# Folding the pooling branch's two weights into one, built on chip and kept in DRAM

## The chip, the cores and the metric

One core of a Trainium2 chip runs the whole model layer. The metric is the device time of one execution in microseconds. Of the kernel before, three runs are shown: 2617.74, 2624.07 and 2628.94, median 2624.07 us.

The engines are named as in the profile: PE (TensorE, matmuls; PEld its weight loads), DVE (VectorE), ACT (ScalarE), POOL (GpSimd) and SP (SyncE, which here only issues transfers). A name with a q behind it, such as SPq or ACTq, is the engine's instruction queue, where transfers are issued.

## The reference

The layer has two mixing branches, a gate on each, an output projection and a feed-forward part. Only the pooling branch changes. Cut to what matters (`u_pool` are the first 512 columns of the input projection, `zg` the gate columns):

```
# pool_mixer: for each of four groups of 128 channels, window w = 2, 4, 8, 16
outs.append(win_sum / count - ug[:, :, g])          # trailing mean minus token
mixed = einsum('bsgc,gcd->bsgd', pooled, pool_w)    # one 128x128 weight per group
mixed = mixed.reshape(B, S, 512) * pool_scale       # one scale per channel
ya = mixed @ w_pa                                   # 512 -> 1024
merged = gates[0] * ya + gates[1] * yb
x = x + merged @ w_o
x = x + conv_glu_ffn(rmsnorm(x))
```

Between the pooled channels and `ya` everything is linear: a block-diagonal 512x512 weight, a scale per channel, and a 512x1024 weight.

## The kernel before

**Precision and operands.** All inputs are 32-bit floats. A product is made of three matmuls in the fp32r type: each factor is split into a high part (a cast, on ACT) and a low part (the difference, on DVE), and high x high, high x low and low x high are accumulated. Activations are split by `split` (L591; cast L597, difference L598). Weights run through `Stream`: an operation of the plan takes one or more raw 256 KB loads (`load`, L176, issued by SP at L182 into 8 buffers, `N_RAW`), may add some of them (in the first mixer, sums of quarters of a weight, on POOL and DVE at L338 and L397), and then converts the result into a high and a low half (`convert`, cast L205 on ACT, difference L206 on DVE) in one of 6 operand buffers (`N_OPS`). `advance` runs the conversions ahead, one at each tick (six counted matmuls, L145), at most four operands (`LOOKAHEAD`) beyond the next to be used. A raw buffer is loaded again only when the last operation that reads it has been converted (`load_ahead`). Sums that the second mixer needs again are stored to DRAM (`keep`, stored at L310 by SP).

**Order of the work.** The sequence of 2048 tokens is worked in two passes of 1024 tokens, each of two blocks of 512. Each pass is `mixer` and then `ffn`. The large products use a seven-product scheme over 2x2 blocks (P1 to P7), with sums of weights and of activations as operands; the activations' forms (B11, T1, T2 and so on) are made by `forms_a_task` and `forms_b_task`, with transposes on PE (L646) and combinations on DVE (L703). `mixer` begins with `proj_io` (inputs and output gates of the recurrent branch), whose products go in the order P1, P2, P6, P5, P7, P4, P3 with four operands each and twelve matmuls per operand. P1 and P2 need one load per operand and no sums; in the first pass P6 needs three loads and two adds per operand (w8 to w11 in the profile's names). P6 needs the form T2, which is made from about P2 on. Then follow 14 units of `PROJ`: kinds fq, g and u, seven operands each. The tasks of the recurrent branch (HGRN) and of pooling run beside them, stepped by the ticks.

**The pooling branch.** The units ("u", 0) and ("u", 1) give the pooled channels' inputs. For each block and group a `pool_task` (L757) makes the windowed mean minus the token into `p` (L774 to L777), splits it (`pl`), multiplies it with the group's 128x128 part of `pool_wt` in three matmuls (L782 to L784) into a PSUM bank `pm`, evicts the bank with the scale on ACT (L786, `mx`) and spills it to DRAM (`md`, by ACT's queue at L791). `pool_wt` is one operand of the stream ("pw"), loaded in each pass before ("u", 0) and held until eight tasks are done. Near the end of the mixer `pa_task` fetches the eight tiles back (L796, by SP), splits them, and `branch("pa", ...)` multiplies them with eight operands of `w_pa` (256 KB each), gates and sums.

**Who orders what.** Each engine works its instructions in order. The program is written in the order described, and a scheduler orders each engine's instructions by a simulated timeline before the run, so an instruction that is ready may stand ahead of one written earlier. Queues are in order: a store that waits on SP holds the loads behind it.

Of the kernel before, what the change touches and what calls it, by code (L numbers as in the profile page):

```python
# [11 lines left out]
F32 = mybir.dt.float32  # L12
F32R = mybir.dt.float32r
U8 = mybir.dt.uint8
AF = mybir.ActivationFunctionType
# [3 lines left out]
P = 128  # L19
SEQ = 2048  # L20
D = 1024
KD = D // P
# [35 lines left out]
M_ORDER = (0, 4, 1, 5, 2, 6, 3, 7)  # L58
# [20 lines left out]
def tile_trunk(  # L79
# [3 lines left out]
    w_in_t: bass.AP,  # L83
    w_io: bass.AP,
    pool_wt: bass.AP,
    w_pa_t: bass.AP,
    w_pb_t: bass.AP,
    w_o: bass.AP,
    w_up_t: bass.AP,
# [6 lines left out]
    pe, act, dve, pool, sp = nc.tensor, nc.scalar, nc.vector, nc.gpsimd, nc.sync  # L96
# [6 lines left out]
    dram = ctx.enter_context(tc.tile_pool(name="dram", bufs=1, space=bass.MemoryType.DRAM))  # L103
    banks = ctx.enter_context(tc.tile_pool(name="banks", bufs=8, space=bass.MemoryType.PSUM))

    def slot(name, cols=TB, dt=F32):
        return slots.tile([P, cols], dt, tag="s", name=name, padded_shape=[P, 528])

    def bank(name, cols=512):
        return banks.tile([P, cols], F32, tag="b", name=name, padded_shape=[P, 512])  # L110

    def f32(ap):
        return ap.bitcast(F32)
# [30 lines left out]
    def mm(*args, **kw):  # L144
        count[1] = pe.matmul(*args, **kw)  # L145
        count[0] += 1
        if count[0] % MM_PER_TICK == 0:
            tick()
# [102 lines left out]
    stream = Stream()  # L251
# [60 lines left out]
    def plan_one(key, src):  # L312
        r = stream.raw(src)
        stream.op(key, lambda nm, r=r: r.tile, [r])
# [3 lines left out]
    def plan_io(b0):  # L318
        for p in IO_ORDER:
            for k in range(4):  # L320

                q = [w_io[k, :, c * 512 : (c + 1) * 512] for c in (0, 3, 1, 2)]
                one = {"P1": 0, "P2": 1, "P4": 3}
                if p in one:
                    plan_one("io", q[one[p]])
                    continue
                if b0:
                    plan_one("io", lambda k=k, p=p: kept["io", k, p])
                    continue
                use = {"P6": (2, 3, 0), "P5": (2, 3), "P7": (2, 0), "P3": (2, 3, 0, 1)}[p]  # L330
                raws = [stream.raw(q[i]) for i in use]

                def fn(nm, k=k, p=p, raws=raws):
                    t = raws[0].tile
                    for i, r in enumerate(raws[1:]):
                        t2 = slot(f"{nm}s{i}")
                        (dve if i == (p == "P6") and p != "P5" and p != "P7" else pool
                         ).tensor_tensor(t2, t, r.tile, ALU.add)  # L338
                        t = t2
                    keep(("io", k, p), t)  # L340
                    return t

                stream.op("io", fn, raws)

    def plan_unit(key, src, kind, i, order, b0):
        mv, mg = proj_tiles(kind, i)
# [8 lines left out]
    def plan_mixer(b0):  # L355
        plan_io(b0)
        for kind, i in PROJ:
            if (kind, i) == ("u", 0):
                plan_one("pw", pool_wt)
            plan_unit("in", w_in_t, kind, i, ORDER, b0)  # L360
        for key, src in (("pa", w_pa_t), ("pb", w_pb_t)):
            for i in range(8):
                plan_one(key, src[i // 2][:, i % 2 * 512 : i % 2 * 512 + 512])
        plan_rows("wo", w_o, R_OUT, KD // 2)

    def proj_tiles(kind, i):
# [155 lines left out]
    o_n1, o_n2, o_bg, o_ps, o_lb, o_hg, o_cb, o_cw = offs  # L522
# [8 lines left out]
    def col(o):  # L531
        return cols[:, o : o + 1]
# [58 lines left out]
    def split(src, name, on_pool=False):  # L591
        hi = slot(name + "h", TB, F32R)
        lo = slot(name + "l", TB, F32R)
        if on_pool:
            pool.tensor_scalar(hi, src, 1.0, 0.0, ALU.mult, ALU.add)
        else:
            act.copy(hi, src)  # L597
        dve.tensor_tensor(lo, src, f32(hi), ALU.subtract)  # L598
        return hi, lo
# [154 lines left out]
        return forms[key]  # L754


    def pool_task(b, g, u, w_mix, md):  # L757
        add = pool if g % 2 == 0 else dve
        w = WINDOWS[g]
        pool.tensor_copy(u[:, 1:16], uhist[:, g, 1:16])  # L760
        pool.tensor_copy(uhist[:, g, 1:16], u[:, 513:528])
        s = u
        k = 1
        lo = 1
        while k < w:
            t = slot(f"s{b}_{g}_{k}", 528)
            lo += k
            a = 16 if 2 * k == w else lo
            add.tensor_tensor(t[:, a:528], s[:, a:528], s[:, a - k : 528 - k], ALU.add)
            s = t  # L770
            k *= 2
            yield 6
        p = slot(f"p{b}_{g}")
        dve.scalar_tensor_tensor(p, s[:, 16:528], 1.0 / w, u[:, 16:528], ALU.mult, ALU.subtract)  # L774
        if b == 0:
            dve.tensor_tensor(p[:, :16], s[:, 16:32], inv[:, g], ALU.mult)
            dve.tensor_tensor(p[:, :16], p[:, :16], u[:, 16:32], ALU.subtract)  # L777
        pl = split(p, f"pl{b}_{g}")
        yield 6
        ps = bank(f"pm{b}_{g}")  # L780
        c = g * P
        pe.matmul(ps, w_mix[:, 0, c : c + P], pl[0], start=True, stop=False)  # L782
        pe.matmul(ps, w_mix[:, 0, c : c + P], pl[1], start=False, stop=False)
        pe.matmul(ps, w_mix[:, 1, c : c + P], pl[0], start=False, stop=True)  # L784
        t = slot(f"mx{b}_{g}")
        act.activation(t, ps, AF.Copy, scale=col(o_ps + g))  # L786
        md[b, g] = spill(t, f"md{b}_{g}")

    def spill(t, name):
        d = dram.tile([P, TB], F32, tag=name, name=name)  # L790
        act.dma_start(d, t)  # L791
        return d
# [307 lines left out]
    def proj_io(b0, forms, late, vd, zd):  # L1100
        bk = {}
        e1, u2, u3 = {}, {}, {}

        def temp(d, key, j):
            d[j] = slot(f"io{b0}_{key}_{j}")
            return d[j]

        def out_v(hf, j, a):
            t = slot(f"v{b0}_{hf}_{j}")
            value(t, a, bk["Y" if hf == 0 else "V"][j])  # L1110
            sp.dma_start(vd[hf][:, j, :], t)

        def out_z(hf, j, a):
            t = slot(f"z{b0}_{hf}_{j}")
            g = slot(f"zs{b0}_{hf}_{j}")
            value(t, a, bk["Z" if hf == 0 else "V"][j])
            act.activation(g, t, AF.Sigmoid)
            (dve if hf == 0 else pool).tensor_tensor(t, t, g, ALU.mult)
            sp.dma_start(zd[hf][:, j, :], t)

        def after(p, j):
            if p == "P1":
                act.copy(temp(e1, "e1", j), bk["X"][j])
            elif p == "P2":
                out_v(0, j, (e1[j], "add"))
            elif p == "P6":
                dve.tensor_tensor(temp(u2, "u2", j), e1[j], bk["Z"][j], ALU.subtract)
            elif p == "P7":
                dve.tensor_tensor(temp(u3, "u3", j), bk["Z"][j], e1[j], ALU.subtract)
                out_z(1, j, (u3[j], "add"))  # L1130
            elif p == "P4":
                out_z(0, j, (e1[j], "from"))
            elif p == "P3":
                out_v(1, j, (u2[j], "sub"))

        for p in IO_ORDER:
            xs = need(forms, FORM[p], late)
            kb = "Y" if p == "P2" else BANK[p]
            if kb not in bk:
                bk[kb] = [bank(f"io{b0}_{kb}_{j}") for j in range(NT)]  # L1140
            for k in range(4):
                if (p, k) == GO_IO[b0 > 0]:
                    go_io[0] = True
                w = stream.get("io")
                for j in range(NT):
                    n_step(bk[kb][j], w, xs[k], j, p in FIRST + ("P2",) and k == 0, k == 3,
                           skip_group_check=True)
                    if k == 3:
                        after(p, j)
                stream.used(1)  # L1150

    def mixer(b0, forms, late):
        vd = [dram.tile([P, NT, 512], F32, tag=f"vd{b0}_{hf}", name=f"vd{b0}_{hf}")
# [3 lines left out]
        md, od, gd = {}, {}, {}  # L1157
# [37 lines left out]
            return emit  # L1195

        held = {}
        pooled = [0]

        def pool_run(hf, g, u):  # L1200
            def gen():
                yield from pool_task(b0 + hf, g, u, held["w"], md)
                pooled[0] += 1
                if pooled[0] == 8:
                    stream.used(1)
            Task(gen())

        def emit_u(i):
            def emit(s, hf, a, ps):
# [44 lines left out]
        emits = {"fq": emit_fq, "u": emit_u, "g": emit_g}  # L1254
        mixed, oT = {}, {}
        for n, (kind, i) in enumerate(PROJ):
            if (kind, i) == ("u", 0):
                held["w"] = stream.get("pw")
            u = Unit(f"{kind[0]}r{b0}_{i}", "in", emits[kind](i))
            for p in ORDER:  # L1260
                u.multiply(p, forms, late)
                u.after(p)
                if n == len(PROJ) - 1 and p == "P1":
                    mtask = Task(pa_task())
# [318 lines left out]
```

## Time and profile before

| what | value |
|---|---|
| median of the three runs | 2624.07 us |
| lowest, highest | 2617.74, 2628.94 us |
| the profiled execution, its own time | 2626.91 us |
| its span | 2625.2 us |
| PE busy | 2537.5 us, 97% of the span, 11464 matmuls and transposes |
| DVE busy | 1977.9 us, 75% |
| ACT, POOL busy | 1170.8 us, 45%; 913.0 us, 35% |
| granted PE clock, mean | 0.987 |
| DMA | 496.90 MB, mean 189 GB/s |

How to read the rows that follow: a group's row gives the line, the engine, the operation, the tile written and the tiles read, the shapes and the count, then busy time and mean. A row for one tile gives minimum, median and maximum of the durations in ns and the first and last start. A row in order of time gives start, length, engine, line and names; the bracket at its end is the idle time ahead of it and who ended it. A row of a stretch gives its borders, its length, and the busy time of PE, PEld, DVE, ACT and POOL with the instructions that started in it, then the granted PE clock as a share of full speed, the busy share of the 16 DMA engines and GB/s. A transfer's row gives who issued it, how often, the size and the median time from issue to landing.

### The profile page before, as it was taken

Reading aid. Unit: us, or ns where it says so; the run is one execution under the profiler, and the core shown is the slowest. Engines: PE = TensorE matmul, PEld = TensorE weight load, DVE = VectorE, ACT = ScalarE, POOL = GpSimd, SP = SyncE. Lnnn points to the kernel's source line nnn. Section 1 sums busy time; section 2 is a strip of 40 time slices with the busy share of each in tenths; the row PEclk is TensorE's granted clock in tenths of the full one; section 3 lists DMA queues with packets and bytes.
Section 4 is the critical chain, followed back from the end, with each engine's and each line's share of the span. In section 5 each row is a group of like instructions: output and inputs, shape, how many; then the busy total and the mean of one; then the engine's idle time right before and its main releaser. Section 6 shows DMA issues by size and latency. Waiting matters only on the chain. (4 is left out here: it accounts for less than half of the span.)

```text
span 2625.2 us, 35598 instructions
## 1 busy us (share of the span) xinstructions
PE 2537.5 (97%) x11464; PEld 2065.1 (79%) x11464; DVE 1977.9 (75%) x3390; ACT 1170.8 (45%) x2204; POOL 913.0 (35%) x1253
## 2 busy tenths in 40 slices
PE   7899999998999999999999999999999999999998
PEld 6688877777778888878878788888787888887887
DVE  7888779458789877877376787775778887777845
ACT  5334334313655454455364344443345454444633
POOL 6544344042444433353141111210623433335402
PEclk8999999999999999999999999999999999999999
DMA  6787759988768897488364344346452444445942
GB/s 213 271 223 205 204 181 245 267 263 209 217 184 244 239 235 211 148 299 282 98 206 159 97 125 133 109 153 213 149 166 88 151 151 148 141 140 182 378 142 105
DMA packets 254059, 496.90 MB, mean 189 GB/s; under 512 B 26736, under 2 KB 43248, under 8 KB 253552
## 3 DMA queue, kind: packets, MB, share of 16 engines
q1 hardware_dynamic: 187968, 319.89, 38.3%
q0 software_dynamic: 41504, 110.64, 16.5%
q10 hardware_dynamic: 24400, 64.08, 7.0%
q8 instruction: 91, 1.49, 0.2%
q14 instruction: 96, 0.79, 0.1%
HBM read 384.94 MB, written 187.17 MB: 218 GB/s over the span
## 5 line engine op out<-in xcount | busy, mean ns | idle before, releaser
L205 ACT CAST ops<-raw 128x512 fp32r<-128x512 f32 x732 | 451.5, 620 | 819.7 <-PE dn_P L145 140.0
L206 DVE TENSOR_TENSOR ops<-raw,ops 128x512 fp32r<-128x512 f32 x732 | 565.2, 776 | 205.3 <-ACT ops L205 194.3
L1375 DVE SCALAR_TENSOR_TENSOR e<-h,cols,e 128x512 f32<-128x512 f32 x176 | 142.6, 813 | 30.2 <-ACT e L1373 26.1
L1373 ACT ACTIVATE e<-h,cols 128x512 f32<-128x512 f32 x176 | 142.5, 814 | 24.2 <-DVE h L978 16.9
L1378 DVE SCALAR_TENSOR_TENSOR e<-h,cols,e 128x512 f32<-128x512 f32 x176 | 133.9, 769 | 3.0
L796 POOL DMA_DIRECT2D g_P<-dg_P x154 | 83.7, 545 | 107.6 <-PE dn_P L145 69.4
L1084 POOL TENSOR_TENSOR gf_P<-e,e 128x512 f32<-128x512 f32 x44 | 67.9, 1545 | 152.9 <-DVE e L1384 97.5
L1295 POOL TENSOR_TENSOR ya<-ya,gl 128x512 f32<-128x512 f32 x32 | 46.8, 1490 | 107.7 <-DVE gl L1287 107.7
L1084 POOL TENSOR_TENSOR gf_P<-gf_P,e 128x512 f32<-128x512 f32 x44 | 60.2, 1368 | 68.0 <-DVE e L1384 67.5
L1368 POOL COPY h<-h 128x2 f32<-128x2 f32 x88 | 40.7, 481 | 114.3 <-DVE h L976 112.3
L1370 POOL COPY hist<-h 128x2 f32<-128x2 f32 x88 | 35.3, 401 | 125.9 <-DVE h L978 124.2
L1382 ACT ACTIVATE e<-e 128x512 f32<-128x512 f32 x88 | 55.6, 631 | 38.8 <-DVE e L1378 38.4
L1191 POOL TENSOR_TENSOR q<-q,qs 128x512 f32<-128x512 f32 x16 | 21.9, 1366 | 141.6 <-ACT qs L1190 72.9
L978 DVE TENSOR_TENSOR h<-up_u,up_V 128x512 f32<-128x512 f32 x88 | 60.1, 684 | 13.6 <-PE up_V L145 13.1
L1228 ACT ACTIVATE gt<-gt,cols 128x512 f32<-128x512 f32 x48 | 34.8, 725 | 77.4 <-DVE gt L978 63.5
L845 POOL COPY qm<-q 128x64 f32<-128x64 f32 x64 | 24.9, 410 | 117.3 <-DVE q L910 31.2
L1060 DVE TENSOR_TENSOR x<-x,wo_P 128x512 f32<-128x512 f32 x88 | 56.6, 689 | 8.2 <-PE wo_P L145 8.2
L1060 DVE TENSOR_TENSOR ac<-ac,dn_P 128x512 f32<-128x512 f32 x72 | 46.6, 684 | 13.4 <-PE dn_P L145 13.3
L1398 POOL DMA_DIRECT2D dg_P<-gf_P x88 | 52.5, 596 | 10.8 <-POOL gf_P L1084 6.5
L853 PE MATMUL pl<-qm,k 128*128 128x192 f32 x256 | 48.2, 331 | 6.1 <-DVE qm L849 3.8
L1444 POOL TENSOR_TENSOR fss<-fss 128x1 f32<-128x1 f32 x16 | 4.6, 288 | 142.0 <-ACT fj L1433 142.0
L853 PEld LDWEIGHTS pl<-qm,k 128*128 128x128 f32 x256 | 43.3, 191 | 10.4 <-ACT qm L844 3.4
(1265 smaller groups left out, 8283.6 us busy)
## 6 DMA issues: line engine op xcount, KB each, us to landing
g_P<-dg_P POOLq DMA_DIRECT2D x154, 256.0 KB, 6.4
raw<-in_w_up_t SPq DMA_DIRECT2D x132, 256.0 KB, 3.2
raw<-in_w_in_t SPq DMA_DIRECT2D x98, 256.0 KB, 3.2
dg_P<-gf_P POOLq DMA_DIRECT2D x88, 256.0 KB, 3.9
raw<-in_w_io SPq DMA_DIRECT2D x68, 256.0 KB, 5.1
dg_P<-e SPq DMA_DIRECT2D x66, 256.0 KB, 3.3
raw<-in_w_dn SPq DMA_DIRECT2D x66, 256.0 KB, 3.0
x<-in_x SPq DMA_DIRECT2D x64, 256.0 KB, 5.3
```

The costliest lines, as they stand in the source:

```text
L205: self.mark = act.copy(hi, v)
L206: dve.tensor_tensor(lo, v, f32(hi), ALU.subtract)
L796: eng.dma_start(t, d)
L853: pe.matmul(pa_[:, c * 192 : c * 192 + 192], ks[:, (i + c) * P : (i + c + 1) * P], mv[:, c].rearrange("p s x -> p (s x)"), start=True, sto ...
L978: dve.tensor_tensor(dst, t, ps, ALU.add if how == "add" else ALU.subtract)
L1060: dve.tensor_tensor(t, t, ps[j], ALU.add if sg > 0 else ALU.subtract)
L1084: pin(pool.tensor_tensor(t, x0, x1, op))
L1373: in_turn(act.activation(t, h[:, 2:], AF.Identity, bias=col(o_cb + mt), scale=col(o_cw + 4 * MF + mt)))
L1375: in_turn(second(dve.scalar_tensor_tensor(t, h[:, 1 : 1 + TB], col(o_cw + 2 * MF + mt), t, ALU.mult, ALU.add)))
L1378: dve.scalar_tensor_tensor(t, h[:, 0:TB], col(o_cw + mt), t, ALU.mult, ALU.add)
L1382: in_turn(act.activation(g, g, AF.Silu))
L1398: pool.dma_start(d, t)
```

## The change

`pool_wt`, the scale and `w_pa` are multiplied once, on the chip, in the first pass. Behind P2 of the first `proj_io`, nine operands are planned: the pooling weight (laid out transposed now), and eight parts of `w_pa` (one for each group and half of the output columns), scaled by ACT as they are made. `make_mix` multiplies them in eight groups of three matmuls, evicts each with an ACT copy, and stores it by SP's queue into a DRAM tile `w_mix`, four pieces of 128 columns for each partition. The pooling tasks spill `p` itself, with no split, matmul, eviction or scale, and the "pa" operands of both passes are read from `w_mix`, in the same order of columns. The "pw" operand ahead of ("u", 0) and its holding are gone.

```diff
@@ plan_io @@
+            if p == "P2" and not b0:
+                plan_mix()
+
+    def plan_mix():
+        plan_one("pw", pool_wt)
+        for g in range(4):
+            for c in range(2):
+                r = stream.raw(w_pa[g][:, c * 512 : (c + 1) * 512])
+
+                def fn(nm, g=g, r=r):
+                    t = slot(f"{nm}s")
+                    act.activation(t, r.tile, AF.Copy, scale=col(o_ps + g))
+                    return t
+
+                stream.op("mix", fn, [r])
+
+    w_mix = dram.tile([P, KD, 512], F32, tag="wmix", name="wmix")
+
+    def make_mix():
+
+        wt = stream.get("pw")
+        for g in range(4):
+            for c in range(2):
+                w = stream.get("mix")
+                ps = bank(f"mix{g}_{c}")
+                a, b = (wt[:, i, g * P : (g + 1) * P] for i in range(2))
+                mm(ps, a, w[:, 0], start=True, stop=False)
+                mm(ps, a, w[:, 1], start=False, stop=False)
+                mm(ps, b, w[:, 0], start=False, stop=True)
+                stream.used(1)
+                t = slot(f"mixs{g}_{c}")
+                act.copy(t, ps)
+                sp.dma_start(w_mix[:, 4 * c : 4 * c + 4, g * P : (g + 1) * P],
+                             t.rearrange("p (m c) -> p m c", m=4))
+        stream.used(1)
@@ plan_mixer @@
-            if (kind, i) == ("u", 0):
-                plan_one("pw", pool_wt)
...
-        for key, src in (("pa", w_pa_t), ("pb", w_pb_t)):
-            for i in range(8):
-                plan_one(key, src[i // 2][:, i % 2 * 512 : i % 2 * 512 + 512])
+        for m in M_ORDER:
+            plan_one("pa", w_mix[:, m])
+        for i in range(8):
+            plan_one("pb", w_pb_t[i // 2][:, i % 2 * 512 : i % 2 * 512 + 512])
@@ pool_task @@
-        pl = split(p, f"pl{b}_{g}")
-        yield 6
-        ps = bank(f"pm{b}_{g}")
-        c = g * P
-        pe.matmul(ps, w_mix[:, 0, c : c + P], pl[0], start=True, stop=False)
-        pe.matmul(ps, w_mix[:, 0, c : c + P], pl[1], start=False, stop=False)
-        pe.matmul(ps, w_mix[:, 1, c : c + P], pl[0], start=False, stop=True)
-        t = slot(f"mx{b}_{g}")
-        act.activation(t, ps, AF.Copy, scale=col(o_ps + g))
-        md[b, g] = spill(t, f"md{b}_{g}")
+        md[b, g] = spill(p, f"md{b}_{g}")
@@ proj_io @@
                 stream.used(1)
+            if p == "P2" and not b0:
+                make_mix()
@@ mixer @@
-        pooled = [0]
...
-            if (kind, i) == ("u", 0):
-                held["w"] = stream.get("pw")
```

More of the change, by code (lines that the diff above doesn't have):

```diff
@@ L85, in tile_trunk @@
     pool_wt: bass.AP,
-    w_pa_t: bass.AP,
+    w_pa: bass.AP,
     w_pb_t: bass.AP,
@@ L1197, in mixer @@
         held = {}
-        pooled = [0]
         def pool_run(hf, g, u):
[L1201 to L1206, printed above, removed]
+            Task(pool_task(b0 + hf, g, u, md))
         def emit_u(i):
@@ L1566 @@
         "w_io": io_of(w_in[:, 1536:2560]),
-        "pool_wt": a["pool_w"][0].transpose(1, 0, 2).reshape(P, 512),
-        "w_pa_t": pairs_of(a["w_pa"][0]),
+        "pool_wt": a["pool_w"][0].transpose(2, 0, 1).reshape(P, 512),
+        "w_pa": a["w_pa"][0].reshape(4, P, 1024),
         "w_pb_t": pairs_of(a["w_pb"][0]),
```

2 lines of the change are left out of this document (1 added, 1 removed).

## The prediction

> **What bounds the kernel now.** I read the busy shares first, then a table of stretches of the span, then the order of time where stretches lose TensorE (PE) time.
>
> ```profile
> PE 2537.5 (97%) x11464; PEld 2065.1 (79%) x11464; DVE 1977.9 (75%) x3390; ACT 1170.8 (45%) x2204; POOL 913.0 (35%) x1253
> ```
> ```profile
> core 0: us, PE busy (x) PEld busy (x) DVE busy (x) ACT busy (x) POOL busy (x), PEclk, DMA share, GB/s
> ...
> 40.00:92.00 52.00, 42.27 (x180) 33.19 (x178) 51.21 (x70) 23.14 (x39) 26.12 (x30) 0.90 0.60 210
> 92.00:124.00 32.00, 28.29 (x113) 21.99 (x114) 28.26 (x30) 11.56 (x20) 25.21 (x17) 0.95 0.77 252
> 124.00:480.00 356.00, 344.28 (x1720) 286.35 (x1721) 287.75 (x668) 133.89 (x300) 143.03 (x149) 0.99 0.77 215
> 480.00:500.00 20.00, 13.65 (x57) 10.58 (x56) 6.99 (x15) 8.03 (x26) 3.72 (x6) 0.86 0.86 301
> ...
> 1480.00:1790.00 310.00, 309.43 (x1592) 260.09 (x1591) 230.79 (x608) 130.08 (x296) 48.57 (x78) 1.00 0.43 130
> ```
>
> Over the whole span it is PE, 97%. But the two places that the change touches are of two kinds. The pooling tasks run in 124 to 480 (first mixer) and in 1480 to 1790 (second). In the second PE is busy 309.43 us of 310, so a matmul less is its time less. In the first it is 344.28 of 356. The new work stands after P2 of the first projection, at about 40 us, and the stretch from 40 to 92 is VectorE's (DVE): busy 51.21 us of 52, while PE stands idle for 52 - 42.27 = 9.7 us. The order of time shows both ends of that stretch:
>
> ```profile
> 39.86 0.63 PE L145 MATMUL io_Y<-ops,x_f7h 128*128 128x512 f32 x2
> ...
> 52.22 1.22 PE L145 MATMUL io_Z<-ops,x_T20h 128*128 128x512 f32 x2 [1.53 <-DVE x_t L703]
> ...
> 92.09 1.19 PE L145 MATMUL io_Z<-ops,x_T40h 128*128 128x512 f32 x2 [3.79 <-DVE io_u L1129]
> ```
>
> P2 ends at 40.6 (its last row is io_Y). P6 begins at 52.22 and P4 at 92.09, and DVE released both. Whatever DVE gets to do before P4 therefore moves P4, and from there on PE is too full (28.29 of 32, then 344.28 of 356) to win it back.
>
> **The change part by part.**
>
> *Taken away: the pooled matmuls.* Each of 16 tasks (8 in each mixer) issues three 128x512 matmuls.
>
> ```profile
> L782 PE MATMUL pm<-pl_0h,ops x4: 387/396/476, 202.9 to 1527.4; 128*128 128x512 f32 x4
> ...
> L597 ACT CAST pl_0h<-p x4: 621/622/625, 198.4 to 1517.3; 128x512 fp32r<-128x512 f32 x4
> L598 DVE TENSOR_TENSOR pl_0l<-p,pl_0h x4: 681/692/693, 199.0 to 1517.9; 128x512 fp32r<-128x512 f32 x4
> ...
> L786 ACT ACTIVATE mx<-pm,cols x16: 669/685/700, 213.8 to 1715.1; 128x512 f32<-128x512 f32 x16
> ```
>
> A matmul's own 396 ns overlaps its neighbours, so the price is the distance from one to the next, from the chain that ended last:
>
> ```profile
> 2065.33 5.58 PE up_Z L145 x24
> ```
>
> That is 5.58/24 = 0.2325 us. 24 matmuls are 5.6 us in each mixer. The second mixer's count in full, the first's at its busy share, 5.6 x 344.28/356 = 5.4. Value **-11.0 us**. Bounds: -5.6, if the first mixer's PE only waits longer for something else, and -17, if half of its 11.7 us of idle goes with the DVE and ACT work below.
>
> *Taken away: the split and the eviction.* 16 x (0.622 + 0.685) = 20.9 us of ACT and 16 x 0.692 = 11.1 us of DVE. PE covers both: neither engine sets the end of those stretches (DVE 287.75 of 356 and 230.79 of 310). If that cover were gone they would be worth up to 11 us, but it is there; I take **-0.5 us** for first-mixer waits, and the ends lie in the bounds above. The spill of the pooled tile now makes ACT's queue wait for DVE's last write of p, with later casts and evictions behind it; the old cast of p was an ACT instruction at the same place with the same wait, so nothing. Its transfer only comes sooner. The branch's weights come from the new DRAM tile instead of an input, in as many rows of 2 KB and the same order: nothing. The first mixer's weight buffer that was held from the first pooling unit to the second is free: nothing, since the look-ahead of four operands stays. The 6.35 us that PE is idle in 480 to 500 belong to the fetch of the pooled tiles and I leave them as they are.
>
> *Added on PE:* 8 groups of 3 matmuls, another 5.6 us, between P2 and P6, where 9.7 us are idle. Covered: **0**, and 5.6 if they come to stand after the wait.
>
> *Added on ACT:* 8 scalings (as L786, 0.685), 9 casts (0.62) and 8 evictions (a copy from PSUM, taken like a cast), some 16 us. ACT is busy 23.14 of 52: covered, 0 on the path.
>
> *Added on DVE:* the low halves of nine operands. Their price has two values in the trace:
>
> ```profile
> 34.43 1.86 DVE L206 TENSOR_TENSOR ops<-w8s,ops 128x512 fp32r<-128x512 f32 x1 [0.73 <-ACT ops L205]
> ...
> 83.44 0.68 DVE L206 TENSOR_TENSOR ops<-w19s,ops 128x512 fp32r<-128x512 f32 x1
> ```
> ```profile
> 34.43 1.31 POOL L338 TENSOR_TENSOR w9s<-raw,raw 128x512 f32<-128x512 f32 x1
> ```
>
> It takes 0.68 us alone and 1.86 when POOL adds at the same moment. DVE has slack before 40, but the look-ahead is four operands: pool_w and three of the eight w_pa parts. These take the place that w8 and w9 (P6's first two, an add and a cast each, so four DVE instructions) have now, so all nine come out as extra work after 40. 9 x 0.68 = 6.1, and POOL is busy for about half of 40 to 92 (26.12 of 52), though not always reading against it: I let two of nine be slow, +2 x 1.18 = 2.4. Value **+8.5 us**. Bounds: nine slow ones, 16.7, and with PE's 5.6 uncovered 22.3; below, -3.0, where all nine find DVE's slack before 40 and the new matmuls keep PE's clock up. That last figure is from these two rows:
>
> ```profile
> 50.00:55.00 5.00, 3.47 (x11) 2.49 (x10) 4.89 (x10) 1.82 (x3) 0.00 (x0) 0.50 0.36 105
> 55.00:60.00 5.00, 5.00 (x18) 3.96 (x17) 4.92 (x10) 2.94 (x6) 0.00 (x0) 0.75 0.28 95
> ```
>
> P6 starts at half clock after the wait: 3.47 x 0.50 + 5.00 x 0.25 = 3.0 us lost.
>
> [...]
>
> *Added and moved on SP and the DMA engines.* Nine 256 KB loads ahead of P6 and eight 256 KB stores of 512-byte pieces.
>
> ```profile
> 16.17 17.52 SPq L182 DMA_DIRECT2D raw<-in_w_io  x11
> ...
> 42.64 8.36 SPq L182 DMA_DIRECT2D raw<-in_w_io  x3
> ```
> ```profile
> raw<-in_w_io SPq DMA_DIRECT2D x68, 256.0 KB, 5.1
> ...
> z<-zd SPq DMA_DIRECT2D x16, 256.0 KB, 4.0
> ```
> ```profile
> 20.00:40.00 20.00, 20.00 (x88) 16.21 (x87) 11.76 (x18) 10.26 (x26) 14.19 (x31) 1.00 0.56 183
> 40.00:60.00 20.00, 13.96 (x59) 10.60 (x58) 19.25 (x33) 7.87 (x14) 8.61 (x18) 0.74 0.29 98
> 60.00:80.00 20.00, 20.00 (x88) 16.20 (x87) 20.00 (x22) 9.85 (x18) 14.55 (x11) 1.00 1.01 357
> ```
>
> 17 x 0.262 MB = 4.5 MB, 12.5 us at the 357 GB/s of 60 to 80. The DMA engines are free for 0.44 x 20 + 0.71 x 20 = 23 us before 60, so there is room. What is lost is the lead: today the eleven loads from 16.17 on bring P6's operands (three loads each) while P1 and P2 run. Now pool_w and w_pa take that place, and each store waits on SP for its eviction, with P6's later loads queued behind it and, behind those, POOL's adds and DVE. P6 is 48 matmuls, 11.1 us, and four operands one load after another are 4 x 5.1 = 20.4: bounds 0 and +9.3. With eight load buffers two to three operands are still ahead, which is nearer to nothing: **+1 us**.
>
> *Sum:* -11.0 - 0.5 + 8.5 + 1.0 = **-2.0 us**. The profiled execution took 2626.91 us (span 2625.2), so 2624.9 by its own time. That execution is 2.8 above the median of the runs shown, 2624.07, from which the same sum gives **2622 us**.
>
> **The rivals.**
>
> *Faster: the start costs nothing.* The scheduler puts the nine operands into DVE's idle 8.2 us of 20 to 40 (11.76 of 20 busy), the matmuls into PE's gap, and P6 starts warm. For it: the loads are needed by nothing else and could be there by 30. Against it: the look-ahead of four, and w8 and w9, which use that slack now. -11.0 - 0.5 - 3.0 = -14.5: 2610 us. [...]
>
> *Slower: P6 starved of operands.* The mechanism is in one place, the queue of operands between P2 and P6: DVE works through T2's forms and P2's evictions first, then the mix operands at the slow price (16.7), PE's mix matmuls come last (5.6), and then P6's operands start without their lead (9.3): 31.6 in all, -11.5 + 31.6 = +20.1: 2644 us. It is slower at all from a start cost of 11.5 on, and by 0.5% from 24.6 on. For it: DVE's 51.21 of 52, and the 8.36 us that SP already takes for three loads at 42.64. Against: work that DVE has finished earlier makes P4's own 3.79 us wait shrink.
>
> *The freed matmuls do not come back in the first mixer.* Its PE then waits for HGRN's DVE chains, and only the second mixer's 5.6 remain: -5.6 + 8.5 + 1.0 = +3.9: 2628 us. For it: DVE is busy 287.75 of 356 there; against: PE 344.28.
>
> **How the numbers follow.** Forecast 0.42 (its own range 2614 to 2632), faster rival 0.24, slower rival 0.22, first mixer gives nothing 0.12. What a measurement of this kernel can tell from no change is about 0.5%, 13.1 us: faster is below 2611, slower above 2637. Three quarters of the faster rival and 0.03 of the forecast lie below: 0.21. Most of the slower rival (0.19) and 0.03 of the others lie above: 0.22. The rest, 0.57, is within. The range 2607 to 2642 leaves out about a tenth on each side.
>
> **What would show it.** P4's first matmul (x_T40h) at 92.1 + 9.5 = about 101 us would bear out the start's cost; at 89 the faster rival, beyond 115 the slower one. From there to the end of the first mixer's projections the distance must shrink by about 5.4 us, and 1480 to 1790 by 5.6 with PE still full. DVE operands for the mix at 0.68 or 1.8 us tell the two prices apart. A P6 with holes between its operands speaks for lost lead. I am wrong if P4 does not move, or if the second mixer is no shorter.

## The result, and the profile after

| | before | after |
|---|---|---|
| median | 2627.42 us (6 runs, 2617.74 to 2628.94) | 2638.57 us (6 runs, 2635.74 to 2641.18) |
| ratio after / before | | 1.0049, 95% interval 1.0036 to 1.0061 |
| the profiled execution, its own time | 2626.91 us | 2638.42 us |
| its span | 2625.2 us | 2636.7 us |

The change makes the kernel slower: by 11.2 us in the medians, by 0.49% in the ratio of all runs. The forecast was 2622 us. The page's line of busy times of the changed kernel:

```profile
PE 2535.4 (96%) x11440; PEld 2060.8 (78%) x11440; DVE 1964.5 (75%) x3381; ACT 1163.3 (44%) x2195; POOL 918.2 (35%) x1253
```

PE, DVE and ACT all have less to do than before, by 2.1, 13.4 and 7.5 us, and the span is 11.5 us longer. So the time went into waiting. The table of stretches of the changed kernel, with the borders of the prediction, shows where:

```profile
40.00:92.00 52.00, 36.30 (x130) 24.84 (x129) 32.02 (x52) 24.69 (x43) 15.26 (x19) 0.74 0.67 209
92.00:124.00 32.00, 27.99 (x109) 22.29 (x109) 28.80 (x32) 15.06 (x26) 20.02 (x14) 0.89 0.66 227
...
124.00:480.00 356.00, 340.02 (x1691) 280.73 (x1690) 290.88 (x664) 125.72 (x289) 165.08 (x160) 1.00 0.79 222
...
1480.00:1790.00 310.00, 306.37 (x1571) 257.62 (x1570) 231.93 (x617) 118.33 (x269) 49.64 (x80) 0.99 0.40 124
```

In the first of them DVE, which had 51.21 us of 52, now has 32.02, and PE, with 24 more matmuls to do, has 36.30 where it had 42.27. Nobody is full there any more, and the granted clock fell from 0.90 to 0.74. That is the picture of engines that wait for one another in turn. (What the later rows cover lies 14 to 21 us later in this kernel's program than in the kernel before, so they are not read row against row.) The order of time on PE in that place:

```profile
49.98 2.93 PE L145 MATMUL mix<-ops,ops 128*128 128x512 f32 x6 [1.23 <-DVE x_t L737]
55.66 0.79 PE L145 MATMUL mix<-ops,ops 128*128 128x512 f32 x1 [2.75 <-ACT ops L205]
57.75 2.75 PE L145 MATMUL mix<-ops,ops 128*128 128x512 f32 x5 [1.30 <-ACT ops L205]
61.94 1.95 PE L145 MATMUL mix<-ops,ops 128*128 128x512 f32 x3 [1.43 <-ACT ops L205]
66.29 3.02 PE L145 MATMUL mix<-ops,ops 128*128 128x512 f32 x6 [2.41 <-ACT ops L205]
71.26 1.95 PE L145 MATMUL mix<-ops,ops 128*128 128x512 f32 x3 [1.95 <-ACT ops L205]
...
113.51 1.19 PE L145 MATMUL io_Z<-ops,x_T40h 128*128 128x512 f32 x2 [4.01 <-DVE io_u L1154]
```

The 24 matmuls of the mix (the multiplication of the two weights) begin at 49.98, 2.2 us before P6 used to begin (52.22), but they take 23.0 us, until P6 begins at 73.01. So P6 is 20.8 us later, and P4, whose first matmul is the last row, 21.4. The list of PE's waits in the same kernel, from 40 to 115 us (total, times, longest), names one cause for the five holes inside the mix:

```profile
PE mix L145 <- ACT ops L205: 9.8, 5, 2.7
```

And ACT, in order of time, two turns of it (L375 evicts a group, L355 scales an operand, L205 casts it):

```profile
59.69 0.59 ACT L375 COPY mixs<-mix 128x512 f32<-128x512 f32 x1 [1.99 <-PE mix L145]
60.17 0.72 ACT L355 ACTIVATE w13s<-raw,cols 128x512 f32<-128x512 f32 x1
60.79 0.57 ACT L375 COPY mixs<-mix 128x512 f32<-128x512 f32 x1
61.26 0.63 ACT L205 CAST ops<-w13s 128x512 fp32r<-128x512 f32 x1
63.92 0.58 ACT L375 COPY mixs<-mix 128x512 f32<-128x512 f32 x1 [2.04 <-PE mix L145]
64.40 0.72 ACT L355 ACTIVATE w14s<-raw,cols 128x512 f32<-128x512 f32 x1
```

The eviction of a group stands on ACT ahead of the cast of an operand that PE needs one or two groups on. ACT waits at L375 for PE's matmuls, and PE waits for the cast that stands behind L375. It is a loop, whose turns carry one or two groups and take 4.2 to 5.0 us (PE's rows at 57.75, 61.94, 66.29 and 71.26). PE's five waits in it, 1.30 to 2.75 us, sum to 9.8. The rest of the 23.0 us, 13.2, is matmuls at half clock, as the stretches of 5 us show for the changed kernel:

```profile
50.00:55.00 5.00, 2.91 (x6) 1.80 (x6) 4.87 (x8) 2.83 (x6) 2.16 (x3) 0.50 0.06 22
...
60.00:65.00 5.00, 2.45 (x5) 0.79 (x3) 0.69 (x1) 2.96 (x6) 0.00 (x0) 0.50 0.98 315
...
70.00:75.00 5.00, 3.74 (x8) 2.73 (x9) 2.60 (x5) 3.42 (x6) 0.00 (x0) 0.50 0.89 255
75.00:80.00 5.00, 4.80 (x20) 3.58 (x20) 1.29 (x2) 0.62 (x1) 2.57 (x2) 0.98 1.03 314
```

The clock is the third number from the end. It is 0.50 from 50 to 75, and back at 0.98 once PE works without holes. DVE, which the forecast made the limit, is nearly idle in 60 to 65 (0.69 us of 5). Its low halves for the mix cost 0.68 to 0.73 us, the quick price, and wait for ACT too, as one group from the changed kernel's list by line and shape (44 to 75 us) shows:

```profile
L206 DVE TENSOR_TENSOR ops<-w16s,ops 128x512 fp32r<-128x512 f32 x1 | 0.7, 693 | 3.1 <-ACT ops L205 3.1
```

Of the 21.4 us, 11.5 are left at the end. From the rows in order of time, after minus before: P4 +21.4; last unit of the first mixer (its first matmul at 455.06 before) +15.1; P4 of the second pass +16.0; last unit of the second mixer (1751.57 before) +14.0; end of the span +11.5. The first mixer gives back 6.3, the second 2.0, what follows the second mixer 2.5, and 0.9 is lost between the mixers.

### The profile page after: what moved, and what is told of

It reads as the page before. It is cut to its first block, busy times and chain, and to the rows that moved or that the text cites. A ratio compares the mean times of both kernels' runs of the same rounds, so it can differ in the third digit from the quotient of the medians.

```text
span 2636.7 us, 35550 instructions
## 1 busy us (share of the span) xinstructions
PE 2535.4 (96%) x11440; PEld 2060.8 (78%) x11440; DVE 1964.5 (75%) x3381; ACT 1163.3 (44%) x2195; POOL 918.2 (35%) x1253
## 5 line engine op out<-in xcount | busy, mean ns | idle before, releaser
L205 ACT CAST ops<-raw 128x512 fp32r<-128x512 f32 x731 | 450.9, 620 | 828.1 <-PE dn_P L145 145.3
L206 DVE TENSOR_TENSOR ops<-raw,ops 128x512 fp32r<-128x512 f32 x731 | 571.2, 785 | 207.5 <-ACT ops L205 202.3
L870 POOL COPY qm<-q 128x64 f32<-128x64 f32 x64 | 27.7, 443 | 113.2 <-DVE q L894 21.4
L1085 DVE TENSOR_TENSOR ac<-ac,dn_P 128x512 f32<-128x512 f32 x72 | 46.6, 683 | 13.3 <-PE dn_P L145 13.2
L1417 POOL DMA_DIRECT2D dg_P<-gf_P x88 | 52.5, 597 | 10.8 <-POOL gf_P L1109 6.6
```

Source lines behind the costliest of these rows:

```text
L205: self.mark = act.copy(hi, v)
L206: dve.tensor_tensor(lo, v, f32(hi), ALU.subtract)
L1085: dve.tensor_tensor(t, t, ps[j], ALU.add if sg > 0 else ALU.subtract)
```

## The experiments

Three questions: what sets the start's 21 us, what the removed matmuls are worth, and why so little. Ratios are to the kernel before, run on the same chip; P6 and P4 are the first matmuls of these products in the first pass.

| run | P6, us | P4, us | median, us | ratio, 95% interval |
|---|---|---|---|---|
| before (profiled) | 52.2 | 92.1 | 2627.42 | |
| after | 73.0 | 113.5 | 2638.57 | 1.0049 (1.0036 to 1.0061) |
| nomix | 51.0 | 91.2 | 2625.84 | 1.0008 (0.9997 to 1.0019) |
| spread | 51.5 | 90.7 | 2626.26 | 1.0005 (0.9996 to 1.0014) |
| evict_lag | 64.0 | 109.3 | 2635.67 | 1.0040 (1.0026 to 1.0055) |
| lag_pool | 67.8 | 108.1 | 2631.97 | 1.0025 (1.0015 to 1.0035) |
| one_load | 71.9 | 111.4 | 2638.94, one run | |
| lag_one_load | 65.3 | 108.6 | 2638.37, one run | |
| half_u0 | 53.3 | 93.2 | 2617.68 | 0.9959 (0.9946 to 0.9972) |
| half_u1 | 52.5 | 92.7 | 2633.09 | 1.0026 (1.0015 to 1.0036) |
| spread_y6 | | 91.4 | 2629.82 | 1.0011 (1.0001 to 1.0021) |
| before_y6 | | 90.5 | 2646.11 | 1.0067 (1.0054 to 1.0080) |
| spread_half | 56.7 | 97.5 | 2638.16 | 1.0051 (1.0039 to 1.0063) |
| late_half | 57.1 | 97.2 | 2633.99 | 1.0036 (1.0022 to 1.0050) |

### nomix: the removal alone

```diff
-            if p == "P2" and not b0:
-                plan_mix()
...
-        for m in M_ORDER:
-            plan_one("pa", w_mix[:, m])
+        for i in range(8):
+            plan_one("pa", w_pa[i // 2][:, i % 2 * 512 : i % 2 * 512 + 512])
```

> The changed kernel without plan_mix and make_mix: the pa operands are loaded straight from w_pa, so the product with pool_w and the scale are left out. It measures what the change takes away, by itself. Theory (both of the start's explanations): P4 of the first pass starts at 92 us as before, and the time is the before's 2627 less what came back behind the start in the changed kernel, 21.4 - 11.5 = 9.9, so about 2617. My recorded sum (48 matmuls, 11.5 us) gives 2616. A rival, that the removed matmuls only filled waits of the recurrent branch's chains, gives 2622 to 2627 (the second mixer 0 to 2 us shorter).

Measured: 1.0008, with 1 inside the interval. That is the rival's time, not the 2616 to 2617 us of the theory. Without the mix P4 is where it was, which puts the whole start cost on the mix. But taking 48 matmuls, 16 splits and 16 evictions out saves nothing that the runs can tell. P4 in order of time in this kernel:

```profile
91.25 1.19 PE L145 MATMUL io_Z<-ops,x_T40h 128*128 128x512 f32 x2 [3.97 <-DVE io_u L1152]
```

### spread: the mix in another place

The weights' plan and the eight groups move from P2's end to the first pass's units, one group behind each of units 2 to 9 (n counts the units).

```diff
+MIX_AT = 2
-            if p == "P2" and not b0:
-                plan_mix()
...
+            if not b0:
+                plan_mix(n)
...
+            if not b0:
+                make_mix(n)
```

> The changed kernel with its eight mix groups moved: one behind each of the first pass's units 2 to 9, planned there in the stream of operands, where the look-ahead of four operands runs over other matmuls. Theory L and R: P4 back at 92 us, no mix group waits as a chain, the eight groups cost their 24 matmuls, 5.6 us at most, and the time is nomix's plus 3 to 6 us: 2620 to 2623, faster than before. Rival: each group's operands and eviction disturb the recurrent branch's chains, time 2627 or more.

Measured: 1.0005, the same as nomix. The 2620 to 2623 us expected, faster than before, did not come. The multiplication itself, one group at a time behind eight units, costs nothing to be seen. The 11 us of the changed kernel are a matter of where the eight groups stand, all in one place at the start. P4 in this kernel, in order of time:

```profile
90.73 0.83 PE L146 MATMUL io_Z<-ops,x_T40h 128*128 128x512 f32 x2 [3.04 <-DVE io_u L1162]
```

### evict_lag: the loop opened

```diff
+MIX_LAG = 3
...
-                t = slot(f"mixs{g}_{c}")
-                act.copy(t, ps)
-                sp.dma_start(w_mix[:, 4 * c : 4 * c + 4, g * P : (g + 1) * P],
-                             t.rearrange("p (m c) -> p m c", m=4))
+                held_ps.append((g, c, ps))
+                if len(held_ps) > MIX_LAG:
+                    evict()
+        while held_ps:
+            evict()
```

> The changed kernel with each mix group evicted three groups later, so that on ACT the next operands' scaling and cast stand ahead of the eviction. Theory L (the loop: eviction waits for PE, the next operand's scaling and cast wait behind it on ACT, PE waits for them): the 9.8 us of PE waits for casts in the mix mostly go, P6 starts at 62 to 65 us instead of 73.0, and the time falls by 7 to 11 us to 2628 to 2632. Theory R (P6's loads have lost their lead and set its start): P6 stays at 71 us or later and the time within 2 us of 2638.6. Theory D (VectorE's added work, my forecast): no change either.

The same work, with each eviction written three groups later. PE in order of time in this kernel:

```profile
47.84 2.93 PE L146 MATMUL mix<-ops,ops 128*128 128x512 f32 x6 [0.93 <-DVE x_t L748]
54.61 0.80 PE L146 MATMUL mix<-ops,ops 128*128 128x512 f32 x1 [3.84 <-ACT ops L206]
57.39 5.78 PE L146 MATMUL mix<-ops,ops 128*128 128x512 f32 x15 [1.98 <-DVE ops L207]
63.39 0.74 PE L146 MATMUL mix<-ops,ops 128*128 128x512 f32 x2 [0.22 <-DVE ops L207]
63.97 1.33 PE L146 MATMUL io_Z<-ops,x_T20h 128*128 128x512 f32 x5
...
109.35 1.19 PE L146 MATMUL io_Z<-ops,x_T40h 128*128 128x512 f32 x2 [5.33 <-DVE io_u L1165]
```

From the third turn on the loop is gone: fifteen matmuls follow one another, and PE waits for ACT's casts once, 3.84 us, instead of five times, 9.8. So the loop is shown. Its size is less than P6's 9.0 us suggest: the mix takes 16.1 us here (47.84 to 63.97) instead of 23.0, so 6.9 us go: 3.8 are waits (6.0 are left, 3.84 for ACT and 2.20 for DVE), and 3.1 are matmul time (the rows of the mix sum to 13.4 us in the changed kernel and to 10.3 here). The other 2.1 us of the 9.0 are an earlier start of the mix, which no run explains. Nor does P4 gain as much, only 4.2: from P6 to P4 it is now 45.4 us, where the kernels before and after have 39.9 and 40.5. Of PE's waits from 40 to 112 us in this kernel, two lie behind P6's start:

```profile
PE io_Z L146 <- DVE io_u L1165: 5.3, 1, 5.3
PE io_Z L146 <- DVE ops L207: 3.9, 2, 3.7
```

P6's own operands are late now (3.9). The median, 2635.67, misses the 2628 to 2632 that the theory of the loop gave, and the ratio's interval overlaps that of the changed kernel, so a gain in time is not shown.

### one_load, lag_one_load, lag_pool: why P6's operands are late

```diff
+        r = stream.raw(w_pa[0][:, 0:512])
...
-                r = stream.raw(w_pa[g][:, c * 512 : (c + 1) * 512])
```

> The changed kernel, but all eight mix operands are made from one and the same load of w_pa (seven loads fewer, another weight than the reference's). P6's loads then have their lead back and the loop on ACT is as it was. Theory L: P6 still starts at 71 to 74 us and the mix matmuls keep their pace of one pair in 4.2 us; the holes inside P6 (0.2 and 1.3 us) go; P4 at 111 to 113. Theory R: P6 starts at 62 to 66 us, P4 at about 102.

Alone (one_load), one load for all eight parts moves P6 by 1.1 us, as theory L expected: with the loop in place its loads hardly matter.

> Late evictions and one load for all eight mix operands, together (another weight than the reference's). Theory L + R (two limits one behind the other: the loop on ACT sets P6's start, and behind it the loads of P6 to P7 set P4): P6 at about 64 us as with late evictions alone, and P4 now at 101 to 105 instead of 109.3. L alone: P4 stays at 109. R alone would have shown in the run with one load and the loop, which it did not.

With the late eviction as well (lag_one_load), P4 is at 108.6, not at 101 to 105: a miss. The edit did not do what it was meant to: the shared buffer stays held until the last of the eight operands is cast, and SP issued no load from 28.8 to 63.1 us. So this run says nothing on the lost lead.

```diff
-            sp.dma_start(w_mix[:, 4 * c : 4 * c + 4, g * P : (g + 1) * P],
+            pool.dma_start(w_mix[:, 4 * c : 4 * c + 4, g * P : (g + 1) * P],
```

> The changed kernel with the evictions three groups late, and its stores of w_mix issued on GpSimd's queue instead of SP's. If the loads of P6's operands are late because they stand behind the stores on SP's queue: P6 starts at 64 us as in the late-evicting run, but P4 at 103 to 105 instead of 109, and the ratio is 1.001 to 1.003. If they are late because the load buffers are held by operands not yet converted: P4 stays at 108 to 110 and the ratio at 1.003 to 1.005.

With the late eviction and the stores on POOL's queue (lag_pool), P6 and P4 in order of time:

```profile
67.79 1.20 PE L146 MATMUL io_Z<-ops,x_T20h 128*128 128x512 f32 x4 [1.60 <-ACT ops L206]
108.09 1.19 PE L146 MATMUL io_Z<-ops,x_T40h 128*128 128x512 f32 x2 [4.12 <-DVE io_u L1165]
```

The distance from P6 to P4 is 40.3 again. But P6 itself starts 3.8 us later than in evict_lag, about as long as PE waited for P6's operands there (3.7), and P4 gains only 1.3. So the run does not show that the stores on SP's queue had held the loads. The trace of evict_lag speaks against it: the wait of 3.7 us hangs on the operand w19 (DVE makes w18's low half behind w19's second add), whose three loads, going by their order, SP issued from 60.7 to 63.3 us, ahead of the four stores that begin at 66.2. From 20 to 112 us loads on SP waited 1.2 us for the evictions, and 12.2, 7.0 and 6.7 us for ACT's scalings of mix operands, which free load buffers. P4 too came out as expected from held load buffers, the ratio as expected from the queue; no run separates the two alone. The profiled execution (2638.78 us) was one of the slowest of this kernel's ten, so its places are to be read with care. In time the form is better than the changed kernel (1.0015 to 1.0035 against 1.0036 to 1.0061). What sets P6 at 64 to 68 rather than 52 is not taken apart further; the 24 matmuls' own 10.3 us are part of it.

### half_u0 and half_u1: where the removed matmuls' time went

In nomix the second mixer, counted from its unit at 1444, runs 5.4 us ahead by its unit at 1701 and then gives back 3.6 (units are named by their start in the kernel before). The order of time on PE in nomix, just there:

```profile
1699.37 0.39 PE L145 MATMUL gr_Z<-x_T20h,ops 128*128 128x512 f32 x1
...
1709.29 1.13 PE L915 MATMUL pl<-q,k 128*128 128x128 f32 x8 [1.43 <-DVE q L843]
1712.07 0.71 PE L145 MATMUL gr_X<-x_f4h,ops 128*128 128x512 f32 x1 [1.65 <-ACT gr_e L1035]
```

and in the kernel before, at the same point of its program:

```profile
1709.55 0.40 PE L782 MATMUL pm<-pl_3h,ops 128*128 128x512 f32 x1
1709.79 0.39 PE L783 MATMUL pm<-pl_3l,ops 128*128 128x512 f32 x1
1710.01 0.40 PE L784 MATMUL pm<-pl_3h,ops 128*128 128x512 f32 x1
1710.25 0.39 PE L145 MATMUL gr_Z<-x_T20h,ops 128*128 128x512 f32 x1
...
1711.62 0.39 PE L782 MATMUL pm<-pl_3h,ops 128*128 128x512 f32 x1
...
1713.68 1.95 PE L892 MATMUL pl<-q,k 128*128 128x128 f32 x16
```

Before, PE does the second pooling unit's last matmuls while DVE and ACT prepare a recurrent head's `q`. Without them PE arrives sooner and waits, and so do the evictions that stand behind `q` on ACT. This is theory F. The missing matmuls are not the whole of it: before, six of them and twelve matmuls of a projection unit (`gr_Z`) stand between the last `fr_V`, which `q` waits for, and the head's `pl`, and in nomix the scheduler has put eleven of the twelve ahead, from 1699.37 on, so one is left. The runs do not separate the two. The two runs below take out one half each: the pooling tasks of groups 0 and 1 (first unit) or 2 and 3 (second unit). The edit of half_u0, in which half_u1 has `g >= 2`:

```diff
+        if g < 2:
+            md[b, g] = spill(p, f"md{b}_{g}")
+            return
         pl = split(p, f"pl{b}_{g}")
```

> The kernel before, with groups 0 and 1 (the first pooling unit) spilled as they are: their split, matmuls, eviction and scale are left out; groups 2 and 3 as before. Theory F (the second pooling unit's matmuls fill a wait of PE for the start of a recurrent head, the first unit's do not): each mixer gets shorter by about 2.7 us, 5 in all, ratio about 0.998, and the second mixer shows no wait for q beside the one at 1457 us. Rival (PE is not the bound in either mixer): ratio 1.000, like the run without any mix.

> The kernel before with groups 2 and 3, the second pooling unit's, spilled as they are: their split, their 12 matmuls in each mixer, their eviction and their scale are left out, which is what the other half of the removal is. Theory F (in the second mixer the second unit's matmuls stand where TensorE waits for a recurrent head's first products, so that what is taken out there comes back as a wait): no gain, ratio 0.999 to 1.001, and in the second mixer's window two waits of q and two of gr_e where the kernel before has one of each. Rival (a matmul removed is a matmul saved, wherever it stands): as fast as the run that left out groups 0 and 1, ratio 0.996.

PE's waits from 1425 to 1783 us, in half_u0 first:

```profile
PE gr_X L145 <- ACT gr_e L1015: 1.6, 1, 1.6
PE pl L895 <- DVE q L823: 1.2, 1, 1.2
```

and in half_u1:

```profile
PE gr_X L145 <- ACT gr_e L1015: 3.3, 2, 1.6
PE pl L895 <- DVE q L823: 2.7, 2, 1.4
```

The kernel before has the one pair (1.6 and 1.2), the changed kernel and nomix have the two (3.3 and 2.6). With the first unit's matmuls gone the second mixer is 4.3 us shorter (from its unit at 1444 to that at 1751, -2.0 to -6.4), and the kernel 0.41% faster, more than the 0.2% expected. Of the 4.3, 1.6 arise by the unit at 1481, before the first removed matmul at 1516, and as much (1.5) arises there in half_u1, so it is not the matmuls'. The 2.8 behind it (-3.6 to -6.4) are the 12 matmuls at 0.2325. In both mixers that would be 5.6 us; the rest of the 0.41%, some 5 us, is not explained. With the second unit's gone the second mixer is 0.7 us longer, and from the unit at 1481 on 2.2 (+5.1 to +7.3). That bears theory F out in the second mixer.

The time of half_u1 was not expected: 0.26% slower, not the same: a miss. Most of it arises in the first mixer, between its units at 218 and 246 us (+3.1 and +11.4 against the kernel before; 5.7 of it comes back by the unit at 455). Theory F does not explain that, for the matmuls taken out stand later, as their row in the kernel before shows (first start 392.4):

```profile
L782 PE MATMUL pm<-pl_2h,ops x4: 389/390/505, 392.4 to 1700.5; 128*128 128x512 f32 x4
```

Up to the unit at 246 PE's instructions are in the same order in both traces, and those of ACT and DVE differ by two swaps and by one. The first 2.2 us of the loss come where an eviction on ACT waits longer for a store to land (first the kernel before, then half_u1):

```profile
213.82 0.69 ACT L786 ACTIVATE mx<-pm,cols 128x512 f32<-128x512 f32 x1 [3.66 <-DMA kwfq1ins<-w56s]
```
```profile
219.08 0.69 ACT L789 ACTIVATE mx<-pm,cols 128x512 f32<-128x512 f32 x1 [5.83 <-DMA kwfq1ins<-w56s]
```

Behind it PE's waits from 200 to 300 us have a group that the kernel before has with 0.6:

```profile
PE pl L856 <- DVE qm L852: 5.1, 2, 2.6
```

Whether the swaps or the execution's own timing made the landing late is open; the twelve executions lie between 2625.13 and 2638.13 us. So in the first mixer the halves do not show what the matmuls had covered. Their sum, -0.41% and +0.26%, is a little below what nomix shows for both (+0.08%, -0.03 to 0.19).

### spread_y6 and before_y6: can the heads be moved instead

```diff
-        yield 3
+        yield 6
```

> The spread kernel with the recurrent head's first products written three ticks later (yield 6 instead of 3 in hgrn_task), so that PE has 18 more matmuls ahead of them. Theory F: the waits of 1.4 us for q and 1.6 us for gr_e at the start of a head go, about 3 us at 1457, 3 to 4 at 1709 and as much in the first mixer; time 5 to 10 us below spread's 2626, about 2618. Rival: the head's later steps are late instead, time as spread or longer.

> The kernel before with the same three ticks, as control. Theory F: only the wait at 1457 us (2.8 us) and the first mixer's go; time 3 to 5 us below 2624.5. If it gains as much as spread_y6 does over spread, the gain is not that of freed matmuls coming back.

The edit is the first pause of each head's task, in ticks. Both missed what theory F gave: with the spread form the ratio is 1.0011, as its rival said, and the kernel before loses 19 us by it. In spread_y6 the waits for `q` are gone from the second mixer, which gains 4.3 us (+7.5 at its P4 to +3.2 at its last projection's end, against the kernel before), but the first mixer loses 8.7 (-0.7 to +8.0). PE's longest waits there, from 118 to 500 us, are for steps further on in the heads' chains:

```profile
PE pl L886 <- DVE qm L882: 4.5, 1, 4.5
PE po L978 <- DVE ss L968: 3.7, 2, 3.4
```

So the wait at a head's start can be moved, but in these two kernels a later start made other steps late.

### spread_half and late_half: only the half that pays

```diff
-        if 0 <= i < 8:
+        if 0 <= i < 4:
...
+            if not i:
+                for g in (2, 3):
+                    act.dma_start(w_mix[:, :, g * P : (g + 1) * P],
+                                  w_pa[g].rearrange("p (m c) -> p m c", m=KD))
...
+        if g < 2:
+            md[b, g] = spill(p, f"md{b}_{g}")
+            return
```

> Only groups 0 and 1 are multiplied into the branch's weight, 12 matmuls in all, two operands' worth each behind the third to sixth unit of the first pass; groups 2 and 3 keep their own mixing, matmuls and scale as in the kernel before, and their rows of the weight are copied in DRAM from w_pa. Theory F, with the spread form's finding that the multiplication costs nothing behind the units: the time of the run that left out groups 0 and 1 (ratio 0.996), so 0.995 to 0.998, with P4's first matmul at 90 to 92 us. Rival (the 12 matmuls, 4 scalings and 4 evictions are paid for in the first pass): 0.998 to 1.000.

Measured 1.0051: a miss. The gain of half_u0 is not there. PE's waits from 200 to 300 us in this kernel begin with

```profile
PE fr_Z L146 <- DVE fr_u L1062: 5.2, 1, 5.2
```

which the kernel before does not have. But spread has the same wait with 6.8 us in its first mixer and is no slower than the kernel before, so the wait alone does not explain the loss.

> As the half-folded run (groups 0 and 1 multiplied into the weight, groups 2 and 3 as before), but with the 12 multiplying matmuls behind the eighth to eleventh unit of the first pass instead of the third to sixth. If that run's loss came from where the multiplication stands, among the units whose heads start next (its unit at 246 us lost 7.6 us against 168): ratio 0.996 to 1.000. If it came from the form itself, wherever the multiplication stands (the copies in DRAM, the third waiting place, the output projection's later start): 1.003 to 1.006.

Behind units 7 to 10 it is 1.0036 (1.0022 to 1.0050), within the rival's range, and the interval overlaps the earlier form's. In the profiled executions both forms also start 5 us late (P4 at 97.5 and 97.2) and lose some 6 us within the first output projection (+6.3 to +12.7 and +0.7 to +6.3 against the kernel before), where PE's first wait for DVE is 9.5 and 9.3 us instead of 6.7. What of the form does that was not separated. Of the forms tried here that leave nothing out none beats the kernel before; the nearest, spread, equals it.

## Why the prediction was wrong

**"Added on ACT ... covered, 0 on the path".** This step failed. It set ACT's added work against the stretch's length (23.14 us busy of 52). ACT has room to the end: 24.69 of 52 in the changed kernel. But its instructions stand in one order, and that order alternates evictions that wait for PE with casts that PE waits for. Not the sum of the work but the turn of the loop sets the time: 9.8 us of waits in place of 0. Opening the loop in evict_lag shortens the mix by 6.9 us, from 23.0 to 16.1; the remaining delay of P6 was not taken apart.

**"Added on PE ... covered: 0, and 5.6 if they come to stand after the wait".** Wrong by more than its bound. The 9.7 us in which PE was idle were not where the matmuls stand: they are the waits around T2's transposes up to 52.22 (0.92, 1.52, 2.07 and 1.53 us) and the 3.79 ahead of P4. With the clock at 0.50 and the holes, the 24 matmuls take 23.0 us from the first to P6, of which 9.8 are waits.

**"Added on DVE ... +8.5".** The wrong mechanism. The forecast let P4 move by 9.5 us through DVE's work; it moved by 21.4 with DVE at 32.02 of 52. The operands cost 0.68 to 0.73, so the choice between the two prices, 0.68 and 1.86, did not come into play: POOL was busy for only 3.43 us of 50 to 75.

**"What is lost is the lead", +1, bounds 0 and 9.3.** Small while the loop is there: two holes inside P6, 1.5 us, and one_load moves P6 by 1.1. In evict_lag it is 45.4 - 39.9 = 5.5 us between P6 and P4, of which 3.9 are waits for P6's operands. That is inside the bounds, above the value. The stores queued ahead of the loads, one of the two reasons given, are not shown as its cause; held load buffers fit the trace better.

**"The second mixer's count in full", 5.6.** This step failed as well. PE was busy 309.43 us of 310, and still the second mixer gave 2.0 in the changed kernel and 1.7 in nomix (+0.7 to -1.0). Being busy is not the same as being what others wait for: the second unit's matmuls ran while PE would otherwise have waited for `q`, and the wait came up when they went and the order changed with them. The first unit's 12 gave their 2.8 in full, in half_u0.

**"The first's at its busy share", 5.4.** By the profiles the distance from P4 to the last unit shrank by 6.3 in the changed kernel, as forecast, but by 2.0 in nomix, with the same matmuls gone. So the agreement is not the forecast's reason. Which part of the 6.3 is a late start that is caught up was not separated. The fetch of the pooled tiles was rightly left "as they are": PE's wait there is 6.9 us in the changed kernel, some 15 us later, against 6.3 before.

**The rivals.** The slower rival had the place right (between P2 and P6), the size of the time nearly (2644 against 2638.6), and the mechanism wrong: DVE's slow price and a full queue. That it came so near is luck: it had the start cost too high (31.6 against 21.4) and the gain behind it too high as well (11.5 against 9.9). The faster rival is out, with P4 at 113.5 instead of 89. That matmuls in the gap keep the clock up, for which it took off 3.0 us, was the author's assumption: in the changed kernel the mix's matmuls stood there, and the clock was 0.50 from 50 to 75 us. In evict_lag P6 did start quick (matmuls 0.23 us apart from 65.14 to 66.53), but 11.8 us late. "The freed matmuls do not come back in the first mixer" was right in kind, but it held the second mixer's share to be sure, and its 2628 left out the loop. With the runs' numbers the sum is: P4 +21.4; given back in the mixers -8.3; between them +0.9; after the second mixer -2.5, which the profile of nomix has as well (-2.8) and which no run explains. Together +11.5.

## What to carry to other kernels

When work is added between two engines that feed each other, write out each engine's order and look for a loop (an eviction that waits for PE ahead of a cast that PE waits for): busy shares say nothing of it, and here each turn took 4.2 to 5.0 us. Work that is taken from an engine at 99% need not be a gain (nomix, 48 matmuls less, is at 1.0008); look at what PE does next after each removed instruction and whether its input would be there. Small removals and shifts among the side tasks moved this kernel by -9 to +19 us (half_u0 and before_y6), so remove and insert by halves, measure each, and look whether a difference begins ahead of the edit, as half_u1's does.

## What the runs showed of the hardware

In the changed kernel the clock stayed at 0.50 from 50 to 75 us, with holes of only 1.30 to 2.75 us between 0.8 to 3.0 us of matmuls. It was 0.98 from 75 to 80, after PE had worked on from 71.26 with no hole longer than 0.20 us. The length of a stretch of work does not settle it alone, for in evict_lag the clock was 0.50 over the 2.93 us of matmuls at 47.84, 1.00 behind them, while PE stood idle, and 0.50 again behind that.

```profile
47.80:51.00 3.20, 2.93 (x6) 1.82 (x6) 3.20 (x4) 1.21 (x2) 1.84 (x3) 0.50 0.12 42
51.30:54.50 3.20, 0.00 (x0) 0.00 (x0) 3.07 (x7) 2.21 (x5) 0.00 (x0) 1.00 0.00 0
54.70:58.00 3.30, 1.32 (x3) 0.70 (x3) 2.84 (x7) 3.30 (x7) 0.00 (x0) 0.50 0.80 235
```

In the changed kernel the clock was 0.50 over the 3.02 us at 66.29, and 0.50 in the idle stretch behind them (69.4 to 71.2). A long hole was not needed for the fall either: from 40 to 50 us PE was never idle there for longer than 1.58 us, and yet the clock was 0.79 in 45 to 50 and 0.50 from there. What sets it is not shown. A price per matmul from a full stretch (0.2325 us, with the clock at 1.00 from 2060 to 2072 us in the kernel before) is little more than half of the price at a clock of 0.50, 0.43 us: six matmuls take 2.93 us in evict_lag's first row and one alone 0.80 in its second, so (2.93 - 0.80) / 5.
